# Last part of the FFN down projection: both column halves per pair of tokens instead of half after half

## The chip, the cores and the metric

The kernel runs on one core of a Trainium2 chip. The metric is the device time of one execution in microseconds. The time before is the median of three runs. The profile is one further execution recorded by the hardware profiler; its times are counted from the start of its own span.

## The reference

A trunk of two layers on 512 tokens of 1024 channels in float32. Each layer is a token-mixing sublayer (dilated attention and retention) followed by a SwiGLU FFN, each with a residual and a LayerNorm behind it. What the change touches is the end of the FFN:

```python
D_MODEL, SEQ, DEPTH, D_FF = 1024, 512, 2, 2816
def _swiglu(x, w_gate, w_up, w_down):
    h = silu(x @ w_gate) * (x @ w_up)          # [512, 2816]
    return h @ w_down                          # [512, 1024]
for l in range(DEPTH):
    mix = _hybrid_mixer(x, ...)
    x = _layer_norm(ALPHA * x + mix, ln1_g[l], ln1_b[l])
    x = _layer_norm(ALPHA * x + _swiglu(x, ...), ln2_g[l], ln2_b[l])
```

## The kernel before

Every float32 matrix product is done as three matmuls in a reduced float32 format: each operand is split into a high part and a remainder (`hilo`, L94 to L96: a cast on ACT writes the high part, a subtraction on DVE writes the low part), and `high*high + high*low + low*high` is accumulated in a PSUM tile. Raw weights come by DMA on SP's queue into the pool `raw` of 8 buffers; their parts go to `whi` and `wlo`, 4 buffers each. PSUM has 8 tiles in rotation.

"Token" below means a block of 128 tokens; there are four, 0 to 3. `xtok` holds the residual stream of the four tokens with channels in the free dimension; `xh` and `xl` hold the two parts of the transposed stream, which every projection of the next layer reads.

The FFN runs in three parts of the hidden dimension. Parts 0 and 1 go through a Strassen-like scheme and are not touched. Part 2 has 6 hidden blocks of 128 (`FPARTS` (16, 22)). Its down projection is plain: the hidden values `ht` are stationary, the weights stream 512 columns at a time. One call of `xstat` covers one half of the 1024 columns, 6 blocks x 3 matmuls = 18 matmuls per token, 72 for four tokens. The first half (`hf=0`) reads `whi`/`wlo` and runs weight by weight with four open PSUM tiles; the second half (`hf=1`) reads its weights from `xs`, a buffer that is free by then (`tail_units`), and runs token by token.

After each (token, half) `residual` (L1184, L1186) adds the PSUM tile to `xtok` and takes its statistics. After a token's second half `norm` follows (L1169 to L1175, with `rstd_of`, L134 to L138): aggregate on DVE, a first pass over 1024 columns, a power on POOL (`ry`, L135), three tiny steps on DVE, a second pass over the columns. In the last layer the second pass is in two pieces of 512, each followed by its DMA to `out`. In layer 0 a DMA on POOL's queue spills the token, and two steps of `to_xT` are put into a queue of side work: for each half of the channels four transposes on PE (L193, tile `px`), the cast to `xh` on ACT, the subtraction to `xl` on DVE and a copy to `xc` on ACT.

The side queue is emptied by `tick`, which is called after every three matmuls; at the rate set here one entry leaves for every two ticks, and entries `nothing` are spacers. The next layer begins with four 24-matmul products on tokens 0 and 1 (`wstat_halves`, 256 columns each, 96 matmuls), which need `xh`, `xl` of both tokens and four weight units (`whi`/`wlo` at L95, L96), and then the same on tokens 2 and 3, ahead of which `need` forces the transposes that are still in the queue. Each engine runs its instructions in the order of its own list; a scheduler merges the streams of the program into these lists.

Of the kernel before, what the change touches and what calls it, by code (L numbers as in the profile page):

```python
# [19 lines left out]
P = 128  # L20
# [3 lines left out]
NI = S // P  # L24
# [31 lines left out]
def hybrid_kernel(ctx, tc, x, rel_bias, w_in, b_in, w_attn_proj, w_ret_proj, w_out,  # L56
# [3 lines left out]
    pe, act, dve, pool = nc.tensor, nc.scalar, nc.vector, nc.gpsimd  # L60
# [22 lines left out]
    def mm(ps, a, b, start, stop):  # L83
        pe.matmul(ps, lhsT=a, rhs=b, start=start, stop=stop, skip_group_check=True)  # L84
# [6 lines left out]
    def psum(name="px"):  # L91
        return psm.tile([P, S], F32, tag="mm", name=name)

    def hilo(src, hi, lo):  # L94
        act.copy(out=hi, in_=src)  # L95
        dve.tensor_tensor(out=lo, in0=src, in1=hi.bitcast(F32), op=ALU.subtract)  # L96

    def raw(name="raw"):
        return rawp.tile([P, 1024], F32, tag="raw", name=name)
# [4 lines left out]
    def rows(w):  # L104
        return w.rearrange("(k p) c -> p k c", p=P)

    def view(t, a, b):
        return t[:, :a * b].rearrange("p (a b) -> p a b", a=a)

    def load(src, a, b):  # L110
        v = view(raw(), a, b)
        for v_, s_ in pieces(v, src):
            nc.sync.dma_start(v_, s_)
        return v

    def pieces(v, src):

        if len(src.shape) == 3:
            return [(v, src)]
        n = src.shape[3]  # L120
        return [(v[:, :, g * n:(g + 1) * n], src[:, :, g]) for g in range(src.shape[2])]

    def unit(v):
        a, b = v.shape[1], v.shape[2]
        h = view(wp.tile([P, 1024], F32R, tag="whi", name="whi"), a, b)
        l = view(wp.tile([P, 1024], F32R, tag="wlo", name="wlo"), a, b)
        hilo(v, h, l)
        return h, l
# [26 lines left out]
    side, rate, credit, awaited = deque(), [1.0], [0.0], [0] * NI  # L155

    def tick(us):

        if side:
            credit[0] += rate[0] * us  # L160
            while side and credit[0] >= 1.0:
                credit[0] -= 1.0
                side.popleft()()
# [16 lines left out]
    STEP = 0.68  # L180


    def to_xT(src, i, cp, late=None):


        awaited[i] = 2
        t_ = slice(i * P, (i + 1) * P)

        def one(hf):
            awaited[i] -= 1  # L190
            px = psum()
            for d in range(4):
                pe.transpose(px[:, d * P:(d + 1) * P], src[:, (4 * hf + d) * P:(4 * hf + d + 1) * P], ident)  # L193
            pv = px.rearrange("p (d t) -> p d t", d=4)
            ks = slice(4 * hf, 4 * hf + 4)
            hilo(pv, xh[:, ks, t_], xl[:, ks, t_])
            if cp is not None:
                o_ = cp[i // 2][hf][:, :, (i % 2) * P:(i % 2 + 1) * P]
                if late is None:
                    act.copy(out=o_, in_=pv)  # L200
                else:
                    late.append(lambda: act.copy(out=o_, in_=pv))

        return [lambda hf=hf: one(hf) for hf in range(2)]
# [15 lines left out]
    def x_copies():  # L220
        return [[view(raw("xc"), 4, 256) for _ in range(2)] for _ in range(2)]
# [54 lines left out]
                    tick(STEP / 2)  # L276
        return pss

    def xstat(units, n, st, evict, token_outer=False):

        ks = [(u, kk) for u in units for kk in range(u[0].shape[1])]
        nk = len(ks)

        def one(ps, j, i):
            (h, l), kk = ks[j]
            sh, sl = st(j, i)
            mm(ps, sh, h[:, kk], j == 0, False)
            mm(ps, sh, l[:, kk], False, False)
            mm(ps, sl, h[:, kk], False, j == nk - 1)
            tick(STEP)  # L290

        if token_outer:
            for i in range(NI):
                ps = psum("ps")[:, :n]
                for j in range(nk):
                    one(ps, j, i)
                evict(i, ps)
        else:
            pss = [psum("ps")[:, :n] for _ in range(NI)]
            for j in range(nk):  # L300
                for i in range(NI):
                    one(pss[i], j, i)
                    if j == nk - 1:
                        evict(i, pss[i])

    def tail_units(raws):

        out_ = []
        for j, r in enumerate(raws):
            v = xs[:, j].rearrange("p h k t -> p h (k t)").rearrange("p h (a b) -> p h a b", a=2)  # L310
            hilo(r, v[:, 0], v[:, 1])
            out_.append((v[:, 0], v[:, 1]))
        return out_
# [204 lines left out]
    spill = drp.tile([S, D], F32, name="spill")  # L518
# [167 lines left out]
    def layer(ly, cp):  # L686
# [80 lines left out]
        with stage("attn") as ap_, stage("attw", 4) as aw:  # L767
# [62 lines left out]
            if ly == 0:  # L830
# [33 lines left out]
                cp = x_copies()  # L864
# [3 lines left out]
                pss = [psum("ps") for _ in tiles]  # L868
# [41 lines left out]
            if ly:  # L910
                pss = wstat_halves([(us, j) for us in us0 for j in range(2)])
# [50 lines left out]
            bias, tail = {}, []  # L962
            load_bias(0)
            for hp in range(HPG // 2):
# [21 lines left out]
                tail = t_  # L986
                pace(25 if hp < 2 else 32)
            n = [nothing]
# [8 lines left out]
        with stage("ret") as rp:  # L997
# [139 lines left out]
            for dp in range(KD // 2):  # L1137
                h, l = was[dp]
# [5 lines left out]
                for e in range(2):  # L1144
                    cs = slice(e * P, (e + 1) * P)
                    ps = psum("ps")
# [9 lines left out]
        xt = fp.tile([P, NI, D], F32, name="xtok")  # L1156
# [8 lines left out]
        def norm(i, dst=None):  # L1165
            xi = xt[:, i]
            g_, b_ = lnp
            mv = sm.tile([P, 2], F32, tag="mv", name="mv")
            dve.bn_aggr(out=mv, in_=stats[i])  # L1169
            rs = rstd_of(mv[:, 1:2])  # L1170
            dve.scalar_tensor_tensor(out=xi, in0=xi, scalar=mv[:, 0:1], in1=g_, op0=ALU.subtract, op1=ALU.mult)
            n = D if dst is None else D // 2
            for c in range(0, D, n):
                o_ = xi[:, c:c + n]
                dve.scalar_tensor_tensor(out=o_, in0=o_, scalar=rs, in1=b_[:, c:c + n], op0=ALU.mult, op1=ALU.add)  # L1175
                if dst is not None:
                    nc.sync.dma_start(dst[:, c:c + n], o_)

        def residual(i, hf, ps, first, last):
            o_ = xt[:, i, hf * 512:(hf + 1) * 512]  # L1180
            if first:
                dve.scalar_tensor_tensor(out=o_, in0=o_, scalar=ALPHA, in1=ps, op0=ALU.mult, op1=ALU.add)
            else:
                dve.tensor_tensor(out=o_, in0=o_, in1=ps, op=ALU.add)  # L1184
            if last:
                dve.bn_stats(out=stats[i][:, hf], in_=o_)  # L1186

        with stage("mp") as mp:
# [10 lines left out]
            for dp in range(KD // 2):  # L1199
# [8 lines left out]
                pss = [psum("ps") for _ in range(2)]  # L1208
# [21 lines left out]
            for hf in range(2):  # L1230
# [6 lines left out]
                raws = [load(wo_l[:, k:k + 2, hf * 512:(hf + 1) * 512], 2, 512) for k in range(0, KD, 2)]  # L1237
# [4 lines left out]
        wg_l, wu_l, wd_l = rows(w_ffn_gate[ly]), rows(w_ffn_up[ly]), rows(w_ffn_down[ly])  # L1242
        final = ly == DEPTH - 1
        cp = []
# [107 lines left out]
        for part, (f0, f1) in enumerate(FPARTS):  # L1352
            last = part == len(FPARTS) - 1
            ht = []
            for f in range(f0, f1, 2):
                ht.append(fo.tile([P, 7, 2, 256], F32R, tag="op", name="ht"))
                if f:
                    ffn_pair(f, ht[-1], not last)
                else:
                    ffn_plain(f, ht[-1])  # L1360
                if f == 2:
                    drain()
            rate[0], credit[0] = 0.5 / STEP, 0.0
            if not last:
                down_blocks(f0, f1, ht, part == 0)
                continue
            lt = fo.tile([P, 2 * D], F32, tag="op", name="lnp")
            ln_par(lt, ln2_g[ly], ln2_b[ly])

            def h_tok(k, i):  # L1370
                t, q = ht[k // 2], 2 * (i // 2) + k % 2
                cs = slice(i % 2 * P, (i % 2 + 1) * P)
                return t[:, q, 0, cs], t[:, q, 1, cs]

            for hf in range(2):
                def evd(i, ps, hf=hf):
                    residual(i, hf, ps, False, True)
                    if hf == 1:
                        norm(i, out[i * P:(i + 1) * P] if final else None)
                        if not final:  # L1380
                            pool.dma_start(spill[i * P:(i + 1) * P], xt[:, i])
                            side.extend([nothing] * (6, 2, 4, 5)[i] + to_xT(xt[:, i], i, cp))

                raws = [load(wd_l[:, a:a + 2, hf * 512:(hf + 1) * 512], 2, 512) for a in range(f0, f1, 2)]
                tail = hf == 1
                if tail and not final:
                    cp.extend(x_copies())
                xstat(tail_units(raws) if tail else [unit(r) for r in raws], 512, h_tok, evd, token_outer=tail)
        fin.close()
        return cp  # L1390

# [59 lines left out]
```

## Time and profile before

| what | value |
|---|---|
| median of 3 runs | 2125.46 us (2123.43 to 2128.12) |
| profiled execution | 2125.37 us, span 2123.3 us |
| PE busy | 2096.5 us, 99% of the span |
| DVE, ACT, POOL busy | 1585.6, 1112.6, 258.3 us |
| mean granted TensorE clock | 0.995 |
| layer 0's touched part | about 1022.7 to 1057 us |
| the last layer's touched part | about 2078 to 2111 us, end of the span 2123.3 us |

Rows of the timeline read: start, duration, engine, line, operation, output<-input, shape, count, and in brackets the idle time of that engine just before and what ended it. A row of the windows reads: stretch, its length, then for each engine its busy time and (count), the granted TensorE clock, the share of the DMA engines, GB/s. Starts of successive instructions on DVE lie a little closer than their durations.

### The profile page before, as it was taken

What the parts mean: (1) busy time and instruction counts of PE and PEld (TensorE: products, weight loads), DVE (VectorE), ACT (ScalarE), POOL (GpSimd) and SP (SyncE); (2) the same over time, 40 slices, a digit from 0 to 9 for tenths busy, and PEclk for the clock granted to TensorE, in tenths of its full rate; (3) what the DMA queues carried; (4) which work ended last, traced back from release to release, by engine and by line L of the source; (5) the groups of instructions that cost most, each with busy time, mean ns of one, the idle gap of its engine ahead of it and who ended that gap; (6) DMA issues with size and microseconds to landing.
All of it is one profiled execution on the core that took longest, in us unless ns stands there. A gap on an engine that the chain in (4) does not pass through costs nothing.

```text
span 2123.3 us, 34880 instructions
## 1 busy us (share of the span) xinstructions
PE 2096.5 (99%) x13818; PEld 1902.2 (90%) x13818; DVE 1585.6 (75%) x2275; ACT 1112.6 (52%) x1723; POOL 258.3 (12%) x265
## 2 busy tenths in 40 slices
PE   9999999999999999999999999999999999999997
PEld 8989888889988898989899898888899889989896
DVE  7666888787744798887677578887867357988876
ACT  5567655555623365555255666555666233655551
POOL 4111111101000101111120111111100001110101
PEclk9999999999999999999999999999999999999999
DMA  7865567677776168867258554758687761686861
GB/s 243 210 166 147 128 152 181 180 184 177 229 265 197 43 160 192 196 178 190 80 148 229 140 138 120 183 149 205 168 193 247 235 198 37 173 201 166 205 182 40
DMA packets 319940, 363.91 MB, mean 171 GB/s; under 512 B 22429, under 2 KB 251969, under 8 KB 319648
## 3 DMA queue, kind: packets, MB, share of 16 engines
q1 hardware_dynamic: 229888, 257.20, 38.6%
q0 software_dynamic: 62608, 91.68, 23.1%
q10 hardware_dynamic: 27280, 12.80, 2.1%
q8 instruction: 108, 1.77, 0.3%
q14 instruction: 56, 0.46, 0.1%
HBM read 335.84 MB, written 28.53 MB: 172 GB/s over the span
## 4 chain that ended last, share of the span: by engine, by line
PE 88%; issue 4%; DVE 3%; DMA 2%; ACT 2%; POOL 1%; SPq 0%; POOLq 0%; DVEq 0%; ACTq 0%
PE ps L84 80%; PE px L84 6%; DMA raw<-in_w_in 1%; DVE wlo L360 1%; PE px L585 1%; PE px L1043 1%; ACT whi L354 1%; POOL ry L135 1%; DMA y_d<-yt 0%; PE px L193 0%; ACT s L575 0%; DVE xtok L1175 0%; PE px L650 0%; DMA exd<-pk 0%; DVE raw L376 0%
## 5 line engine op out<-in xcount | busy, mean ns | idle before, releaser
L354 ACT CAST whi<-raw 128x1024 fp32r<-128x1024 f32 (+1 forms) x518 | 519.6, 1008 | 461.8 <-PE ps L84 190.0
L360 DVE TENSOR_TENSOR wlo<-raw,whi 128x1024 fp32r<-128x1024 f32 (+1 forms) x518 | 604.7, 1171 | 207.9 <-ACT whi L354 202.1
L84 PE MATMUL ps<-xs,whi 128*128 128x256 f32 (+1 forms) x2944 | 572.1, 293 | 0.4 <-ACT sn L815 0.4
L84 PEld LDWEIGHTS ps<-xs,whi 128*128 128x128 f32 x2944 | 467.6, 191 | 15.0 <-issue 1.7
L84 PE MATMUL ps<-xs,wlo 128*128 128x256 f32 (+1 forms) x1472 | 430.2, 292 | 0.6 <-DVE wlo L360 0.6
L84 PE MATMUL ps<-xh,whi 128*128 128x256 f32 (+1 forms) x1424 | 423.8, 299 | 5.8 <-ACT whi L95 4.0
L84 PE MATMUL ps<-xh,wlo 128*128 128x256 f32 (+1 forms) x1424 | 419.9, 296 | 2.2 <-DVE wlo L96 2.1
L84 PE MATMUL ps<-xl,whi 128*128 128x256 f32 (+1 forms) x1424 | 420.8, 296 | 0.3 <-DVE ve L134 0.3
L84 PEld LDWEIGHTS ps<-xh,whi 128*128 128x128 f32 x1424 | 272.2, 192 | 19.2 <-ACT whi L95 4.9
L84 PEld LDWEIGHTS ps<-xs,wlo 128*128 128x128 f32 x1472 | 281.7, 191 | 6.1 <-DVE wlo L360 1.1
L84 PEld LDWEIGHTS ps<-xl,whi 128*128 128x128 f32 x1424 | 273.5, 192 | 8.8 <-DVE xl L96 0.6
L84 PEld LDWEIGHTS ps<-xh,wlo 128*128 128x128 f32 x1424 | 272.8, 192 | 9.1 <-DVE wlo L96 2.4
L84 PE MATMUL ps<-whi,xs 128*128 128x512 f32 (+1 forms) x768 | 225.0, 362 | 1.0 <-ACT sn L499 1.0
L345 POOL DMA_DIRECT2D raw<-in_w_in x80 | 98.7, 1248 | 692.2 <-DMA raw<-in_w_in 265.4
L96 DVE TENSOR_TENSOR wlo<-raw,whi 128x1024 fp32r<-128x1024 f32 (+2 forms) x78 | 88.8, 1140 | 125.1 <-ACT whi L95 125.0
L376 DVE TENSOR_TENSOR raw<-raw 128x1024 f32<-128x1024 f32 (+1 forms) x148 | 173.9, 1175 | 8.8 <-DMA raw<-in_w_in 6.7
L84 PE MATMUL ps<-whi,ht 128*128 128x512 f32 x544 | 169.1, 390 | 0.0
L84 PEld LDWEIGHTS ps<-whi,xs 128*128 128x128 f32 x768 | 137.8, 188 | 20.5 <-ACT sn L499 1.2
L95 ACT CAST whi<-raw 128x1024 fp32r<-128x1024 f32 (+2 forms) x78 | 76.4, 982 | 142.8 <-PE ps L84 100.3
L84 PE MATMUL ps<-wlo,xs 128*128 128x512 f32 (+1 forms) x384 | 138.3, 360 | 0.1
L84 PEld LDWEIGHTS ps<-whi,ht 128*128 128x128 f32 x544 | 101.8, 188 | 22.4 <-DVE ht L96 1.5
L345 POOL DMA_DIRECT2D raw<-in_w_ffn_gate x40 | 51.7, 1292 | 528.2 <-DMA raw<-in_w_ffn_up 222.7
(221 smaller groups left out, 2975.8 us busy)
## 6 DMA issues: line engine op xcount, KB each, us to landing
raw<-in_w_in SPq DMA_DIRECT2D x168, 512.0 KB, 5.1
raw<-in_w_in POOLq DMA_DIRECT2D x64, 512.0 KB, 8.2
raw<-in_w_ffn_up SPq DMA_DIRECT2D x64, 512.0 KB, 4.8
raw<-in_w_ffn_down SPq DMA_DIRECT2D x52, 512.0 KB, 4.5
raw<-in_w_ffn_gate SPq DMA_DIRECT2D x44, 512.0 KB, 5.4
raw<-in_w_ffn_gate POOLq DMA_DIRECT2D x40, 512.0 KB, 7.6
raw<-in_w_ret_proj SPq DMA_DIRECT2D x32, 512.0 KB, 6.2
raw<-in_w_in SPq DMA_DIRECT2D x56, 256.0 KB, 5.0
```

Source lines behind the costliest of these rows:

```text
L84: pe.matmul(ps, lhsT=a, rhs=b, start=start, stop=stop, skip_group_check=True)
L95: act.copy(out=hi, in_=src)
L96: dve.tensor_tensor(out=lo, in0=src, in1=hi.bitcast(F32), op=ALU.subtract)
L135: pool.tensor_tensor(out=y, in0=ve, in1=mhalf, op=ALU.pow)
L345: pool.dma_start(r, self.src({"P1": "B12", "P3": "B22"}[n], u), accum_op=ALU.add)
L354: act.copy(out=h, in_=src)
L360: dve.tensor_tensor(out=l, in0=src, in1=h.bitcast(F32), op=ALU.subtract)
L376: dve.tensor_tensor(out=r, in0=r, in1=self.t["B22" if n == "P2" else "B21", u], op=ALU.add)
L585: pe.transpose(px[:, hh, j * P:(j + 1) * P], ss[od][:, hh, j * P:(j + 1) * P], ident)
L1043: pe.transpose(px[:, t * P:(t + 1) * P], ys[i][:, t * P:(t + 1) * P], ident)
```

## The change

`xstat` gets a list of tokens. All six weight loads of both halves are now written ahead of the first matmul, and both sets of units are held through the whole part. The order of (half, tokens) is:

- layer 0: half 0 of tokens 0 and 1 together, half 1 of token 0, half 1 of token 1, half 0 of tokens 2 and 3 together, half 1 of token 2, half 1 of token 3;
- last layer: the same up to token 1, then half 0 and half 1 of token 2, then half 0 and half 1 of token 3.

The number of matmuls, casts, subtractions and DMAs stays. The spacers for tokens 2 and 3 change from 4 and 5 to 6 and 3. The out projection, which calls the same `xstat`, keeps its order.

```diff
-    def xstat(units, n, st, evict, token_outer=False):
+    def xstat(units, n, st, evict, token_outer=False, toks=range(NI)):
...
+        groups = [(i,) for i in toks] if token_outer else [toks]
+        for group in groups:
+            ps = {i: psum("ps")[:, :n] for i in group}
             for j in range(nk):
+                (h, l), kk = ks[j]
+                for i in group:
+                    sh, sl = st(j, i)
+                    mm(ps[i], sh, h[:, kk], j == 0, False)
+                    mm(ps[i], sh, l[:, kk], False, False)
+                    mm(ps[i], sl, h[:, kk], False, j == nk - 1)
+                    tick(STEP)
                     if j == nk - 1:
+                        evict(i, ps[i])
...
-            for hf in range(2):
-                def evd(i, ps, hf=hf):
-                    residual(i, hf, ps, False, True)
...
-                            side.extend([nothing] * (6, 2, 4, 5)[i] + to_xT(xt[:, i], i, cp))
-
-                raws = [load(wd_l[:, a:a + 2, hf * 512:(hf + 1) * 512], 2, 512) for a in range(f0, f1, 2)]
-                tail = hf == 1
-                if tail and not final:
-                    cp.extend(x_copies())
-                xstat(tail_units(raws) if tail else [unit(r) for r in raws], 512, h_tok, evd, token_outer=tail)
+            def evd(hf, i, ps):
+                residual(i, hf, ps, False, True)
+                if hf == 1:
+                    norm(i, out[i * P:(i + 1) * P] if final else None)
+                    if not final:
+                        pool.dma_start(spill[i * P:(i + 1) * P], xt[:, i])
+                        side.extend([nothing] * (6, 2, 6, 3)[i] + to_xT(xt[:, i], i, cp))
+
+            raws = [[load(wd_l[:, a:a + 2, hf * 512:(hf + 1) * 512], 2, 512) for a in range(f0, f1, 2)] for hf in range(2)]
+            units = [[unit(r) for r in raws[0]], tail_units(raws[1])]
+            if not final:
+                cp.extend(x_copies())
+            ends = ((0, (2, 3)), (1, (2,)), (1, (3,))) if not final else ((0, (2,)), (1, (2,)), (0, (3,)), (1, (3,)))
+            for hf, toks in ((0, (0, 1)), (1, (0,)), (1, (1,))) + ends:
+                xstat(units[hf], 512, h_tok, lambda i, ps, hf=hf: evd(hf, i, ps), toks=toks)
```

In the changed file all lines below `xstat` stand 9 lower in number (L1184 becomes L1175, L1175 becomes L1166, L1171 becomes L1162, L1169 becomes L1160). On ACT and DVE the casts and subtractions of all six units stood ahead of the part's first residual before as well, and their rows have not moved; SP's and POOL's lists and ACT's, but for one pair of neighbours, are the same.

On PE, at the end of layer 0, before: the last 72 matmuls on `xs`, with the transposes of token 0 among them and those of token 1 behind them, then layer 1's first matmuls (`xh`, `xl` with `whi`):

```order
L84 MATMUL ps<-whi,ht 128x512
L84 MATMUL ps<-xs,ht 128x512 x60
L193 MATMUL px<-ident,xtok 128x128 x4
L84 MATMUL ps<-xs,ht 128x512 x6
L193 MATMUL px<-ident,xtok 128x128 x4
L84 MATMUL ps<-xs,ht 128x512 x6
L193 MATMUL px<-ident,xtok 128x128 x8
L84 MATMUL ps<-xh,whi 128x256
```

PE at the same place now: these are token 2 (18 matmuls) and token 3 (18), and the transposes are those of token 1; token 0's stand further up, within half 0 of tokens 2 and 3:

```order
L84 MATMUL ps<-wlo,ht 128x512
L84 MATMUL ps<-whi,ht 128x512
L84 MATMUL ps<-xs,ht 128x512 x12
L193 MATMUL px<-ident,xtok 128x128 x4
L84 MATMUL ps<-xs,ht 128x512 x6
L193 MATMUL px<-ident,xtok 128x128 x4
L84 MATMUL ps<-xs,ht 128x512 x18
L84 MATMUL ps<-xh,whi 128x256
L84 MATMUL ps<-xl,whi 128x256
L84 MATMUL ps<-xh,wlo 128x256
```

No transpose is left between the part and layer 1. Token 2's two groups of transposes now stand 48 and 60 matmuls behind layer 1's first one, token 3's behind the 96th; before, token 2's stood behind the 60th and the 72nd.

On DVE, before, from the residual of token 2 (half 1) on, the first weight remainder (`wlo`) of layer 1 comes seven rows below the end of this piece:

```order
L1184 TENSOR_TENSOR xtok<-xtok,ps 128x512
L1186 BN_STATS stats<-xtok 128x6
L96 TENSOR_TENSOR xl<-px,xh 128x4x128
L1169 BN_AGGR mv<-stats 128x2
L134 TENSOR_SCALAR ve<-mv 128x1
L1171 SCALAR_TENSOR_TENSOR xtok<-xtok,mv,lnp 128x1024
L136 SCALAR_TENSOR_TENSOR rt<-ry,ve 128x1
L96 TENSOR_TENSOR xl<-px,xh 128x4x128
L137 TENSOR_SCALAR rt<-rt 128x1
L1184 TENSOR_TENSOR xtok<-xtok,ps 128x512
L138 TENSOR_TENSOR ry<-ry,rt 128x1
L1186 BN_STATS stats<-xtok 128x6
```

DVE now, from the same residual on:

```order
L1175 TENSOR_TENSOR xtok<-xtok,ps 128x512
L96 TENSOR_TENSOR wlo<-raw,whi 128x1024
L96 TENSOR_TENSOR xl<-px,xh 128x4x128
L1177 BN_STATS stats<-xtok 128x6
L96 TENSOR_TENSOR wlo<-raw,whi 128x1024
L1160 BN_AGGR mv<-stats 128x2
L96 TENSOR_TENSOR wlo<-raw,whi 128x1024
L134 TENSOR_SCALAR ve<-mv 128x1
L1162 SCALAR_TENSOR_TENSOR xtok<-xtok,mv,lnp 128x1024
L136 SCALAR_TENSOR_TENSOR rt<-ry,ve 128x1
L1175 TENSOR_TENSOR xtok<-xtok,ps 128x512
L137 TENSOR_SCALAR rt<-rt 128x1
```

All four `wlo` (the fourth follows at once) moved ahead of the end of token 2's norm, one `xl` moved out of it.

On DVE at the end of the last layer, before, the residual of token 3 (the row L1184) stands inside the norm of token 2:

```order
L1171 SCALAR_TENSOR_TENSOR xtok<-xtok,mv,lnp 128x1024
L136 SCALAR_TENSOR_TENSOR rt<-ry,ve 128x1
L1184 TENSOR_TENSOR xtok<-xtok,ps 128x512
L137 TENSOR_SCALAR rt<-rt 128x1
L1186 BN_STATS stats<-xtok 128x6
L138 TENSOR_TENSOR ry<-ry,rt 128x1
L1169 BN_AGGR mv<-stats 128x2
L1175 SCALAR_TENSOR_TENSOR xtok<-xtok,ry,lnp 128x512 x2
L134 TENSOR_SCALAR ve<-mv 128x1
L1171 SCALAR_TENSOR_TENSOR xtok<-xtok,mv,lnp 128x1024
```

DVE there now:

```order
L1162 SCALAR_TENSOR_TENSOR xtok<-xtok,mv,lnp 128x1024
L136 SCALAR_TENSOR_TENSOR rt<-ry,ve 128x1
L137 TENSOR_SCALAR rt<-rt 128x1
L138 TENSOR_TENSOR ry<-ry,rt 128x1
L1166 SCALAR_TENSOR_TENSOR xtok<-xtok,ry,lnp 128x512 x2
L1175 TENSOR_TENSOR xtok<-xtok,ps 128x512
L1177 BN_STATS stats<-xtok 128x6
L1175 TENSOR_TENSOR xtok<-xtok,ps 128x512
L1177 BN_STATS stats<-xtok 128x6
L1160 BN_AGGR mv<-stats 128x2
```

Token 2's norm now ends before the two residuals of token 3 (half 0, then half 1).

More of the change, by code (lines that the diff above doesn't have):

```diff
@@ L277, in wstat_halves @@
         return pss
-    def xstat(units, n, st, evict, token_outer=False):
+    def xstat(units, n, st, evict, token_outer=False, toks=range(NI)):
         ks = [(u, kk) for u in units for kk in range(u[0].shape[1])]
         nk = len(ks)
[L284 to L299, printed above, removed]
-            for j in range(nk):
-                for i in range(NI):
-                    one(pss[i], j, i)
+        groups = [(i,) for i in toks] if token_outer else [toks]
+        for group in groups:
+            ps = {i: psum("ps")[:, :n] for i in group}
+            for j in range(nk):
+                (h, l), kk = ks[j]
[5 more added lines that the diff above has]
+                    tick(STEP)
                     if j == nk - 1:
-                        evict(i, pss[i])
+                        evict(i, ps[i])
     def tail_units(raws):
@@ L1373, in h_tok @@
                 return t[:, q, 0, cs], t[:, q, 1, cs]
-            for hf in range(2):
-                def evd(i, ps, hf=hf):
-                    residual(i, hf, ps, False, True)
[L1378 to L1381, printed above, removed]
-                            side.extend([nothing] * (6, 2, 4, 5)[i] + to_xT(xt[:, i], i, cp))
-                raws = [load(wd_l[:, a:a + 2, hf * 512:(hf + 1) * 512], 2, 512) for a in range(f0, f1, 2)]
-                tail = hf == 1
-                if tail and not final:
-                    cp.extend(x_copies())
-                xstat(tail_units(raws) if tail else [unit(r) for r in raws], 512, h_tok, evd, token_outer=tail)
+            def evd(hf, i, ps):
[12 more added lines that the diff above has]
+                xstat(units[hf], 512, h_tok, lambda i, ps, hf=hf: evd(hf, i, ps), toks=toks)
         fin.close()
```

## The prediction

> **What bounds the kernel now.** I read the page first, then the waits of PE over the whole span:
>
> ```profile
> PE 2096.5 (99%) x13818; PEld 1902.2 (90%) x13818; DVE 1585.6 (75%) x2275; ACT 1112.6 (52%) x1723; POOL 258.3 (12%) x265
> PE ps L84 <- ACT whi L95: 4.0, 1, 4.0
> PE ps L84 <- DVE wlo L96: 2.1, 1, 2.1
> PE px L585 <- DVE nm L572: 1.3, 1, 1.3
> ```
>
> PE is the bound, and of what it lost to others the two longest waits happened once each; the next inside the span, in layer 1's attention, is 1.3 us. The number of matmuls does not change, so time can only come from places where PE stands still, runs at a lower clock, or has finished. The windows show where that is near the touched code:
>
> ```profile
> 1057.00:1061.30 4.30, 0.32 (x3) 0.08 (x1) 3.84 (x9) 2.60 (x5) 0.90 (x1) 1.00 0.00 0
> 1061.30:1068.90 7.60, 5.12 (x21) 4.63 (x22) 7.14 (x13) 4.01 (x5) 2.51 (x3) 0.56 0.45 147
> 2110.00:2116.00 6.00, 0.91 (x4) 0.41 (x3) 5.49 (x15) 0.00 (x0) 1.52 (x1) 0.79 0.23 87
> 2116.00:2123.30 7.30, 0.00 (x0) 0.00 (x0) 3.11 (x6) 0.00 (x0) 1.52 (x1) 0.50 0.39 145
> ```
>
> After the first touched part PE (first busy column) is idle for 4.3 us and then works at a clock of 0.56 while DVE (third) is full. After the second it has ended at about 2110.9 and the rest of the span is DVE's norms and the output. These are the handover and the tail; the change acts on both. The handover in PE's timeline:
>
> ```profile
> 1022.68 0.40 PE L84 MATMUL ps<-whi,ht 128*128 128x512 f32 x1
> 1039.03 13.77 PE L84 MATMUL ps<-xs,ht 128*128 128x512 f32 x60
> 1052.63 0.60 PE L193 MATMUL px<-ident,xtok 128*128 128x128 f32 x4
> 1052.98 1.63 PE L84 MATMUL ps<-xs,ht 128*128 128x512 f32 x6
> 1056.28 1.04 PE L193 MATMUL px<-ident,xtok 128*128 128x128 f32 x8
> 1061.35 0.38 PE L84 MATMUL ps<-xh,whi 128*128 128x256 f32 x1 [4.03 <-ACT whi L95]
> 1073.38 0.28 PE L84 MATMUL ps<-xl,whi 128*128 128x256 f32 x1
> 1073.50 0.28 PE L84 MATMUL ps<-xh,wlo 128*128 128x256 f32 x1
> 1078.81 1.03 PE L193 MATMUL px<-ident,xtok 128*128 128x128 f32 x8
> 1080.08 0.74 PE L84 MATMUL ps<-xh,whi 128*128 128x256 f32 x4 [0.24 <-ACT xh L95]
> ```
>
> 72 matmuls from 1022.68 to 1039.03 make 0.227 us each for 512 columns; a step at 256 columns is 0.12 at full clock; a group of four transposes takes 0.35 (1052.63 to 1052.98). Tokens 2 and 3 of layer 1 begin at 1080.08, which is 1.27 after the last transposes begin. That start is my yardstick: behind it nothing is reordered, and of the waits above only the 1.3 us lies there.
>
> **Part 1: PE up to layer 1.** Layer 0's part keeps its 144 matmuls; now four transpose groups stand inside it. Counting from 1022.68 at 0.227: token 0 ends after 54 matmuls at 1034.9, token 1 after 72 at 1039.0, half 0 of tokens 2 and 3 with two transpose groups at 1047.9, token 2 at 1052.3, token 3 at 1056.8. Before, PE was through at about the same time, 1056.28 plus two groups, so nothing is gained up to here.
>
> **Part 2: tokens 0 and 1 are in time.** A token's residual and norm on DVE, and the passage from transposes to `xl`:
>
> ```profile
> 1043.31 0.69 DVE L1184 TENSOR_TENSOR xtok<-xtok,ps 128x512 f32<-128x512 f32 x1 [1.17 <-PE ps L84]
> 1048.65 0.68 DVE L1184 TENSOR_TENSOR xtok<-xtok,ps 128x512 f32<-128x512 f32 x1
> 1073.62 0.60 PE L193 MATMUL px<-ident,xtok 128*128 128x128 f32 x4
> 1074.26 0.59 ACT L95 CAST xh<-px 128x512 fp32r<-128x512 f32 x1 [6.96 <-PE px L193]
> 1074.87 0.69 DVE L96 TENSOR_TENSOR xl<-px,xh 128x512 fp32r<-128x512 f32 x1 [4.48 <-ACT xh L95]
> 1060.23 1.07 ACT L95 CAST whi<-raw 128x1024 fp32r<-128x1024 f32 x1
> ```
>
> One norm is 5.34 (1043.31 to 1048.65); the residual starts some 0.2 after the matmul (90 matmuls end at 1043.1). Tokens 0 and 1 are normed at 1035.1 + 5.3 = 1040.5 and 1045.8. Their transposes come at 1044.5, 1046.2, 1050.6 and 1052.3, so PE does not wait. From transposes to the cast on ACT pass 0.64, to `xl` 1.25. ACT casts token 1's first half at 1051.3, then the first `whi` at 1051.8 to 1052.9, and copies and casts on. On DVE token 2's residual comes at 1052.5, the first `wlo` (about 1.15 each) at 1053.1 to 1054.2, the last `xl` to 1054.9, statistics, the second `wlo` to 1056.7. Layer 1's first matmul at 1056.8 finds its operands; the second unit is wanted 12 matmuls later. The 4.0 and 2.1 us waits go, and with them the low clock behind them.
>
> **Part 3: what is late next.** Token 2's transposes stand 48 matmuls into layer 1, at 1056.8 + 48 x 0.12 = 1062.5, and PE runs in order. Token 2's norm on DVE:
>
> ```profile
> 1053.99 0.68 DVE L1184 TENSOR_TENSOR xtok<-xtok,ps 128x512 f32<-128x512 f32 x1
> 1060.06 1.27 DVE L1175 SCALAR_TENSOR_TENSOR xtok<-xtok,ry,lnp 128x1024 f32<-128x1024 f32 x1
> 1061.24 0.20 DVE L1169 BATCH_NORM_AGGREGATE mv<-stats 128x2 f32<-128x12 f32 x1
> 1068.04 2.35 DVE L96 TENSOR_TENSOR wlo<-raw,whi 128x1024 fp32r<-128x1024 f32 x2
> ```
>
> Before it took 1053.99 to 1061.3 = 7.3, with two `xl`, token 3's residual and statistics inside. Now it starts at 1052.5, loses one `xl` (0.6) and gains four `wlo` (2.35 for two, 4.7): 1052.5 + 7.3 - 0.6 + 4.7 = 1063.9. PE waits about 1.4 us there. Bounds: 0, if the `wlo` fill DVE's wait for POOL's power inside the chain and the steps lie closer; 3, if each step waits for its `whi` from ACT. I take 1.4, the sum of the rows. Behind the waiting transposes stand only layer 1's matmuls; DVE's next `xl` waits for them, with token 3's second norm pass behind it: two `xl`-like passages at most, until about 1068.3.
>
> Then 0.35 + 12 x 0.12 + 0.35 + 36 x 0.12 = 6.5 bring PE to token 3's transposes at 1070.4, which finds token 3 ready, and 1.27 later, at 1071.7, tokens 2 and 3 begin. **Handover: 1080.08 - 1071.7 = 8.4 us gained**, 9.8 without the stall.
>
> Does the stall cost clock as well? A nearby case:
>
> ```profile
> 1207.06 0.33 PE L585 MATMUL px<-ident,s 128*128 128x128 f32 x1 [1.30 <-DVE nm L572]
> 1207.93 0.93 PE L585 MATMUL px<-ident,s 128*128 128x128 f32 x5 [0.55 <-ACT s L575]
> 1208.00:1212.00 4.00, 4.00 (x24) 0.61 0.00 0
> 1212.00:1216.00 4.00, 4.00 (x38) 0.96 0.44 131
> ```
>
> Waits of 1.30 and 0.55 close together were followed by a clock of 0.61 over 4 us: 4 x 0.39 + 4 x 0.04 = 1.7 us of full clock lost. My stall is single and has dense matmuls on both sides, so I take no loss and keep 1.7 as the upper end. The Trainium skill, "TensorE: Matmul & The Clock Gate", section "What's actually happening", says that the clock is halved only after at least one idle window of about 3.4 us; by that rule my stall would cost itself alone, and the sum would stay. The rows above, with 1.85 us of waits in all, do not bear out so long a threshold, which is why I keep the other end.
>
> **Part 4: the weights held, and the pairs.** With two tokens per weight, each unit is used up in 12 matmuls instead of 24, so the third unit and the last hidden block are wanted at 24 x 0.227 = 5.4 us, the first `xs` unit at 8.2, counted from the first matmul (1022.68, or 2078.08 in the last layer). Their last writers:
>
> ```profile
> 1022.75 1.22 DVE L96 TENSOR_TENSOR xs<-raw,xs 128x1024 fp32r<-128x1024 f32 x1
> 1025.85 0.69 DVE L96 TENSOR_TENSOR ht<-sn,ht 128x512 fp32r<-128x512 f32 x1 [0.69 <-ACT ht L95]
> ```
>
> `ht` is complete at 1026.5, wanted at 1028.1; `xs` at 1024.0, wanted at 1030.9. Nothing waits, cost zero; the cover is 1.6 us. Loads and casts were that early before, so holding them moves no DMA; the next layer's `whi` buffers come free at 1047.9 at the latest instead of 1039, ahead of the cast at about 1051.8. The spacers change only where the transposes stand, and that is counted above.
>
> **Part 5: the tail.** The end of the last layer on DVE, and PE's last matmuls:
>
> ```profile
> 2094.42 16.48 PE L84 MATMUL ps<-xs,ht 128*128 128x512 f32 x72
> 2098.70 0.69 DVE L1184 TENSOR_TENSOR xtok<-xtok,ps 128x512 f32<-128x512 f32 x1 [1.17 <-PE ps L84]
> 2102.84 1.41 DVE L1175 SCALAR_TENSOR_TENSOR xtok<-xtok,ry,lnp 128x512 f32<-128x512 f32 x2
> 2112.97 0.68 DVE L1184 TENSOR_TENSOR xtok<-xtok,ps 128x512 f32<-128x512 f32 x1
> 2118.24 1.42 DVE L1175 SCALAR_TENSOR_TENSOR xtok<-xtok,ry,lnp 128x512 f32<-128x512 f32 x2
> ```
>
> PE gives a token every 4.1 us (18 x 0.227), a norm takes 5.5 (4.14 from the residual to the last pass, and its 1.41), so DVE falls behind: token 3's residual starts at 2112.97, though PE ended at 2110.9, and its chain to the last pass takes 5.27 with token 2's steps inside, against 4.14 for token 0 (2098.70 to 2102.84). Now token 2 ends 36 matmuls ahead of the end, at 2102.6; token 1's norm, begun at 2096.0, is through at 2102.1; token 2's is through at 2108.3, then 1.3 for half 0 of token 3, and DVE waits at 2111.0. The last pass starts at 2111.0 + 4.14 = 2115.1 instead of 2118.24. What follows, two pieces and their DMAs, stays. **Tail: 3.1 us gained.** Bounds: 2.0 (only the late start, the chain stays at 5.27) to 3.2.
>
> **Sum.** 8.4 + 3.1 = 11.5 against the profiled execution of 2125.37 (span 2123.3, 2.07 around it): 2113.9. That execution stands 0.09 below the median, which changes nothing at this size.
>
> **The rivals.**
> - The stall is longer or pulls the clock down. For it: the 1207 rows, and DVE full in the handover. Against it: dense matmuls on both sides. Price 1.7 alone, to 1.6 + 1.7 with the 3 us bound: 2115.6 to 2117.2. Chance 0.25.
> - No stall: 2113.9 - 1.4 = 2112.5. Against it is the sum of DVE's rows. Chance 0.1.
> - The handover does not move, since something other than the norms ends last there (weights of layer 1, say), and only the tail is gained: 2125.4 - 3.1 = 2122.3. For it: PE's wait was ended by `whi`, a weight cast. Against it: in ACT's list this cast stands behind the casts of the transposed tokens, and these come early now. Chance 0.07.
>
> The fourth ends on the other side. The second half of the columns already ran in groups of 18 matmuls, one PSUM tile each; its window (the clock is the third number from the end):
>
> ```profile
> 1039.00:1052.60 13.60, 13.60 (x61) 11.21 (x60) 11.12 (x23) 0.00 (x0) 3.65 (x3) 1.00 0.10 39
> ```
>
> - Slower, by the clock: PE's stream is now cut into 6 and 7 groups. If every group cost a spell like the one at 1208, 13 x 1.7 = 22 us would go and the time would be 2136; it decides from 7 such spells on, which eat the 11.5. Against it is the full clock of this window. Chance 0.03.
>
> The Trainium skill has a rule for this rival on the same page, section "A second HAM failure mode: psum-queue depth-cycling": short idles between groups that cycle through PSUM banks make the clock swing. By it the part might run at changing clocks and the time come near 2136; the window above shows no such thing for groups of that size.
>
> **How the numbers follow.** The forecast with its own range of 2112.9 to 2115.2 has 0.5, the rivals 0.25, 0.1, 0.07 and 0.03, and 0.05 goes to small new waits in both parts, 2116 to 2120. About 0.2% (4.3 us) is what a measurement of this kernel can tell from no change. Faster by more than that, below 2121.2, are all but the last rivals: 0.9; 2122.3 counts as the same: 0.07; slower 0.03. The range 2111.8 to 2117.8 leaves out the cases of 0.07 and 0.03 and most of the small new waits, and adds half a microsecond for the runs' spread.
>
> **What would show it.** Right: in PE's timeline no idle ahead of layer 1's first matmul and a clock of 1.00 from 1057 on; one wait of 1 to 2 us at the transposes of token 2, put down to `xtok` or DVE's L1166; tokens 2 and 3 of layer 1 begin near 1071.7; the last residual starts within 0.3 us of the last matmul and the span ends near 2111.8. Wrong: a wait inside the down projection on `ht` or `xs`, a stall of 3 us or more in the handover, or a clock under 1 behind it; or the handover gain given back by new waits in layer 1.

## The result, and the profile after

The changed kernel takes 2112.22 us in the median (2111.05 to 2115.39, six runs) against 2125.01 for the kernel before on the same occasion; the ratio of the two is 0.9946, with a 95% interval of 0.9936 to 0.9956. A run of the kernel before that took 5851.41 us here, and one of 2550.49 us beside the last experiment, are left out of the ratios. The ratio makes 11.5 us (9.3 to 13.6), where 11.5 were forecast; the plain difference of the medians is 12.8. The time lies in the range. The page's line of busy times, and two of PE's waits, the longest one inside the layers and the one at token 2's transposes:

```profile
PE 2092.2 (99%) x13818; PEld 1898.8 (90%) x13818; DVE 1585.8 (75%) x2275; ACT 1112.6 (53%) x1723; POOL 258.3 (12%) x265
PE px L576 <- DVE nm L563: 1.7, 2, 1.5
PE px L193 <- DVE xtok L1166: 0.7, 1, 0.7
```

The 4.0 and 2.1 us waits on layer 1's first weights are gone; one new wait of 0.7, on token 2's norm, is there. The windows of the handover and of the tail:

```profile
1057.00:1061.30 4.30, 4.27 (x36) 4.06 (x34) 3.84 (x8) 0.00 (x0) 1.03 (x1) 1.00 0.71 219
1061.30:1068.90 7.60, 6.91 (x59) 6.91 (x60) 5.02 (x10) 2.25 (x4) 3.79 (x6) 1.00 0.57 206
2098.00:2104.00 6.00, 3.23 (x15) 2.34 (x13) 4.56 (x8) 0.00 (x0) 0.81 (x1) 1.00 0.23 87
2104.00:2110.40 6.40, 0.00 (x0) 0.00 (x0) 2.25 (x6) 0.00 (x0) 0.71 (x1) 0.70 0.22 83
```

In the stretch where PE was idle it is now busy for 4.27 of 4.30 us, and the clock stays at 1.00 behind it (it was 0.56). PE's timeline through the handover:

```profile
1020.79 0.40 PE L84 MATMUL ps<-whi,ht 128*128 128x512 f32 x1
1042.58 0.60 PE L193 MATMUL px<-ident,xtok 128*128 128x128 f32 x4
1042.93 0.48 PE L84 MATMUL ps<-whi,ht 128*128 128x512 f32 x1
1044.40 0.60 PE L193 MATMUL px<-ident,xtok 128*128 128x128 f32 x4
1050.79 0.60 PE L193 MATMUL px<-ident,xtok 128*128 128x128 f32 x4
1055.36 0.28 PE L84 MATMUL ps<-xh,whi 128*128 128x256 f32 x1
1061.99 0.66 PE L193 MATMUL px<-ident,xtok 128*128 128x128 f32 x4 [0.72 <-DVE xtok L1166]
1068.67 1.03 PE L193 MATMUL px<-ident,xtok 128*128 128x128 f32 x8
1069.94 0.74 PE L84 MATMUL ps<-xh,whi 128*128 128x256 f32 x4 [0.24 <-ACT xh L95]
```

Layer 1 begins (1055.36) right behind the part's last matmul, without a wait in brackets. The yardstick, from the part's first matmul to the start of tokens 2 and 3 in layer 1, is 1069.94 - 1020.79 = 49.15 us; before it was 1080.08 - 1022.68 = 57.40. Token 2's norm on DVE, from its residual to the step behind its last pass:

```profile
1050.99 0.69 DVE L1175 TENSOR_TENSOR xtok<-xtok,ps 128x512 f32<-128x512 f32 x1
1060.67 1.27 DVE L1166 SCALAR_TENSOR_TENSOR xtok<-xtok,ry,lnp 128x1024 f32<-128x1024 f32 x1
1061.85 0.20 DVE L1160 BATCH_NORM_AGGREGATE mv<-stats 128x2 f32<-128x12 f32 x1
```

It takes 10.9 us, most of it other work in between (four `wlo`, one `xl`, token 3's residual and statistics), and ends at 1061.9, when PE's transposes start. The tail, on PE and DVE:

```profile
2068.40 0.40 PE L84 MATMUL ps<-whi,ht 128*128 128x512 f32 x1
2096.99 4.24 PE L84 MATMUL ps<-xs,ht 128*128 128x512 f32 x18
2097.22 1.42 DVE L1166 SCALAR_TENSOR_TENSOR xtok<-xtok,ry,lnp 128x512 f32<-128x512 f32 x2
2101.27 0.69 DVE L1175 TENSOR_TENSOR xtok<-xtok,ps 128x512 f32<-128x512 f32 x1 [1.31 <-PE ps L84]
2105.38 1.42 DVE L1166 SCALAR_TENSOR_TENSOR xtok<-xtok,ry,lnp 128x512 f32<-128x512 f32 x2
```

Token 2's last pass (2097.22) is over before PE ends at 2101.2; DVE then waits for PE (1.31 in brackets), which it did not before, and the last pass follows 4.11 behind the residual instead of 5.27. From the part's first matmul to the end of the span are 2110.4 - 2068.40 = 42.0 us against 2123.3 - 2078.08 = 45.2, where the first matmul before is this row:

```profile
2078.08 0.40 PE L84 MATMUL ps<-whi,ht 128*128 128x512 f32 x1
```

The profiled executions in four stretches, in us, divided at the part's first matmul in layer 0, the start of tokens 2 and 3 in layer 1, and the part's first matmul in the last layer:

| kernel | ahead | handover | layer 1 | tail | span |
|---|---|---|---|---|---|
| before | 1022.7 | 57.40 | 998.0 | 45.2 | 2123.3 |
| changed | 1020.8 | 49.15 | 998.5 | 42.0 | 2110.4 |
| difference | -1.9 | -8.25 | +0.5 | -3.2 | -12.9 |

1.4 us of this pair's 12.9 lie outside the handover and the tail.

### The profile page after: what moved, and what is told of

It is laid out like the page before. It is cut to its first block, busy times and chain, and to the rows that moved or that the text cites. A ratio compares the mean times of both kernels' runs of the same rounds, so it can differ in the third digit from the quotient of the medians.

```text
span 2110.4 us, 34883 instructions
## 1 busy us (share of the span) xinstructions
PE 2092.2 (99%) x13818; PEld 1898.8 (90%) x13818; DVE 1585.8 (75%) x2275; ACT 1112.6 (53%) x1723; POOL 258.3 (12%) x265
## 4 chain that ended last, share of the span: by engine, by line
PE 89%; issue 4%; DVE 2%; DMA 2%; ACT 1%; POOL 0%; SPq 0%; POOLq 0%; ACTq 0%; DVEq 0%
PE ps L84 81%; PE px L84 6%; DMA raw<-in_w_in 1%; PE px L576 1%; DVE wlo L351 1%; PE px L1034 1%; ACT whi L345 1%; PE px L193 0%; DMA mb<-exd 0%; ACT s L566 0%; DMA raw<-in_w_ffn_gate 0%; POOL ry L135 0%; PE px L641 0%; DMA exd<-pk 0%; DVE raw L367 0%
```

## The experiments

My theory was that two separate gains add up: in the handover, tokens 0 and 1 are normed while PE still works on tokens 2 and 3, and in the tail, token 2's norm is over when PE ends. The rivals were a single cause, a gain by the held weights and the pairs as such, and a gain given back inside layer 1.

**The last layer alone.** Layer 0 keeps the old order:

```diff
+            order = ((0, (0, 1, 2, 3)), (1, (0,)), (1, (1,)), (1, (2,)), (1, (3,))) if not final else <as changed>
-                        side.extend([nothing] * (6, 2, 6, 3)[i] + ...)
+                        side.extend([nothing] * (6, 2, 4, 5)[i] + ...)
```

> The new order in the last layer alone; layer 0 keeps half after half with its old spacers. The yardsticks are read from the profile: the handover, from the first matmul of layer 0's last down projection to the first matmul of layer 1 on tokens 2 and 3 (57.4 us before, 49.15 in the changed kernel), and the tail, from the first matmul of the last layer's part to the end of the span (45.2 before, 42.0 changed). Theory (two gains that do not depend on each other): handover 57.4, tail 42.0, time 3.2 us under the kernel before, ratio 0.9985. Rival (the gain has one cause, the handover, and the tail is only the spread between runs): tail 45.2, ratio 1.000.

Measured: ratio 0.9985 (0.9976 to 0.9994), 3.2 us. The marks in PE's timeline, with a span of 2120.1:

```profile
1022.23 0.40 PE L84 MATMUL ps<-whi,ht 128*128 128x512 f32 x1
1079.83 0.74 PE L84 MATMUL ps<-xh,whi 128*128 128x256 f32 x4 [0.24 <-ACT xh L95]
2078.05 0.40 PE L84 MATMUL ps<-whi,ht 128*128 128x512 f32 x1
```

Handover 57.6, tail 42.05: the tail's gain stands by itself.

**Layer 0 alone.** The last layer keeps the old order:

```diff
+            order = <as changed> if not final else ((0, (0, 1, 2, 3)), (1, (0,)), (1, (1,)), (1, (2,)), (1, (3,)))
```

> The new order in layer 0 alone; the last layer keeps half after half. Theory: handover 49.15, tail 45.2, time 8.3 us under the kernel before, ratio 0.9961. Rival (the changed kernel's whole 12.9 us, with the 1.4 us that lie outside the two parts, belongs to this change): 9.7 us, ratio 0.9954. Rival (part of the gain is given back by new waits inside layer 1): the stretch from the second yardstick to the last layer's part over 999.5 us, against 998.0 before and 998.5 changed.

Measured: ratio 0.9964 (0.9950 to 0.9977), 7.6 us with an interval from 4.9 to 10.6, which holds the theory's 8.3 and the first rival's 9.7 alike; the stretches decide. Span 2112.8:

```profile
1020.93 0.40 PE L84 MATMUL ps<-whi,ht 128*128 128x512 f32 x1
1070.08 0.74 PE L84 MATMUL ps<-xh,whi 128*128 128x256 f32 x4 [0.24 <-ACT xh L95]
2067.72 0.40 PE L84 MATMUL ps<-whi,ht 128*128 128x512 f32 x1
```

Handover 49.15, layer 1 997.6, tail 45.1. Layer 1 is no longer than before, so nothing beyond the spread of its length (last section) is given back there, and 8.25 + 3.2 = 11.45 is the sum of the two.

**The pairs swapped in layer 0.** Tokens 2 and 3 first, 0 and 1 last; the groups and the time for which weights are held stay:

```diff
+            for hf, toks in (<as changed> if final else
+                             ((0, (2, 3)), (1, (2,)), (1, (3,)), (0, (0, 1)), (1, (0,)), (1, (1,)))):
```

> The changed kernel with the pairs swapped in layer 0: tokens 2 and 3 first, tokens 0 and 1 last, all else the same, the weights held as long. Theory (the gain of the handover is that tokens 0 and 1, which layer 1 reads first, are normed while PE still works on the others): it is lost and more, PE idles some 12 us ahead of layer 1 and runs at half clock behind it, handover 62 (59 to 65), against 57.4 before. Rival (the gain is that of holding the weights and of groups by pairs): 49 to 52.

Measured: one run, 2126.23, beside 2127.27 of the kernel before. PE's marks:

```profile
1021.75 0.40 PE L84 MATMUL ps<-whi,ht 128*128 128x512 f32 x1
1062.03 1.94 PE L193 MATMUL px<-ident,xtok 128*128 128x128 f32 x8 [5.55 <-DVE mv L1160]
1068.73 1.97 PE L193 MATMUL px<-ident,xtok 128*128 128x128 f32 x8 [4.76 <-DVE xtok L1166]
1070.53 1.01 PE L84 MATMUL ps<-xh,whi 128*128 128x256 f32 x3
2082.34 0.40 PE L84 MATMUL ps<-whi,ht 128*128 128x512 f32 x1
```

PE waits 5.55 and 4.76 us for the norms of tokens 0 and 1, and the mean clock from 1058 to 1070 is 0.54. No transposes mark the start of tokens 2 and 3 here. Counted in PE's list, the 97th matmul of layer 1 starts at 1083.06, which makes the handover 61.3. Taken from the other side, 1060.6 us pass from the first part's first matmul to the last part's, against 1055.4 before and 1047.6 changed, so with some 998 for layer 1 it is about 62.5. Either is longer than before and within what was expected. The held weights and the pairs are not the gain; which tokens end first is.

**Token 2's transposes 12 matmuls later.** In layer 1's products `tick` counts half, so one spacer is worth 12 matmuls there and not six.

```diff
-                        side.extend([nothing] * (6, 2, 6, 3)[i] + ...)
+                        side.extend([nothing] * (6, 2, 7, 2)[i] + ...)
```

> The changed kernel with one spacer more ahead of token 2's transposes and one less ahead of token 3's, which puts token 2's transposes 60 and 72 matmuls into layer 1 instead of 48 and 60. Theory (PE's stall there is only the order of PE's list against the end of token 2's norm): the wait on the norm goes, handover 48.2 to 48.4. Rival (DVE is the bound of the whole handover, and the wait reappears at token 3's transposes): handover 49.1 with a wait at the 96th matmul.

```profile
1019.54 0.40 PE L84 MATMUL ps<-whi,ht 128*128 128x512 f32 x1
1061.30 0.60 PE L193 MATMUL px<-ident,xtok 128*128 128x128 f32 x4
1067.76 0.74 PE L84 MATMUL ps<-xh,whi 128*128 128x256 f32 x4 [0.24 <-ACT xh L95]
```

The wait is gone and the handover is 48.22 (one run, 2109.88 us). The stall comes from the place of these transposes in PE's list, ahead of the end of token 2's norm.

**Token 2's transposes 24 matmuls earlier.**

```diff
-                        side.extend([nothing] * (6, 2, 6, 3)[i] + ...)
+                        side.extend([nothing] * (6, 2, 4, 5)[i] + ...)
```

> The changed kernel with two spacers less ahead of token 2's transposes (4 instead of 6) and two more ahead of token 3's: token 2's transposes now stand 24 and 36 matmuls into layer 1, 2.9 us earlier on PE, while token 2's norm ends when it did. Theory: PE's single stall there grows from 0.9 to 3.8 us; if a stall of that length leaves the clock alone, the handover is 52.0 us (49.15 + 2.9); if the clock falls to a half for one spell as behind the 1.30 and 0.55 us waits (1.7 us lost), 53.7. Rival (the stall is another engine's work that moves with the transposes): handover 49.2.

PE's marks and its windows (busy, count, clock, DMA share, GB/s) of one run, 2119.53 us:

```profile
1023.88 0.40 PE L84 MATMUL ps<-whi,ht 128*128 128x512 f32 x1
1065.17 0.85 PE L193 MATMUL px<-ident,xtok 128*128 128x128 f32 x4 [3.69 <-DVE mv L1160]
1077.52 0.74 PE L84 MATMUL ps<-xh,whi 128*128 128x256 f32 x4 [0.24 <-ACT xh L95]
1064.00:1066.00 2.00, 0.83 (x5) 0.86 0.78 212
1066.00:1068.00 2.00, 2.00 (x12) 0.50 0.81 308
1068.00:1070.00 2.00, 2.00 (x15) 0.79 0.03 12
```

Handover 53.64, the figure for a spell of low clock. It is 4.49 longer than in the changed kernel, and the longer stall (3.69 against 0.72) makes 2.97 of that. The other 1.5 go with the low clock behind the stall, for which the windows allow at most 2 x (0.14 + 0.50 + 0.21) = 1.7 us. That is what the first rival of the prediction would have cost. The change did not pay it: in none of the four profiles with a stall of 0.7 at this place is the clock under 1 behind it.

**The last layer's order in layer 0.**

```diff
+            order = ((0, (0, 1)), (1, (0,)), (1, (1,)), (0, (2,)), (1, (2,)), (0, (3,)), (1, (3,)))
```

> The changed kernel with the last layer's order in layer 0 as well: half 0 and half 1 of token 2, then half 0 and half 1 of token 3. Token 2 ends 36 matmuls ahead of the end, and its norm on DVE stands ahead of layer 1's four weight remainders instead of behind them. Theory (the stall is those four subtractions in the norm): no wait at token 2's transposes, handover 48.2 to 48.5. Rival (the remainders are now late and PE waits for them at layer 1's start): handover 49.5 to 51 with a wait on wlo.

```profile
1023.23 0.40 PE L84 MATMUL ps<-whi,ht 128*128 128x512 f32 x1
1060.25 0.38 PE L84 MATMUL ps<-xh,wlo 128*128 128x256 f32 x1 [0.63 <-DVE wlo L96]
1072.32 0.74 PE L84 MATMUL ps<-xh,whi 128*128 128x256 f32 x4 [0.24 <-ACT xh L95]
PE ps L84 <- ACT sn L490: 1.7, 1, 1.7
```

Handover 49.09 (one run, 2117.62 us). The wait at the transposes is gone as the theory has it, but the rival was right that another takes its place, 0.63 on a weight remainder that now stands behind the norm. Neither had the size: 48.2 to 48.5 was too low, 49.5 to 51 too high. I had summed DVE's rows for token 2 alone there and had not asked what its norm pushes back. One of the two, the norm or the remainders, is late on DVE in either order. This run's layer 1 is 1001.2 us long, with a wait of 1.7 in its value projection (last row); see the last section.

**Layer 0's order in the last layer.**

```diff
+            ends = ((0, (2, 3)), (1, (2,)), (1, (3,)))
```

> The changed kernel with layer 0's order in the last layer too: half 0 of tokens 2 and 3 together, then half 1 of token 2, half 1 of token 3. Token 2 now ends 18 matmuls (4.1 us) ahead of the end instead of 36, less than a norm's 5.5. Theory (the tail is set by the norm of token 2 still running when PE ends): token 3's last residual starts about 1.5 us after PE's end, tail 43.5 (43.2 to 43.8). Rival (the tail is set by PE's end alone): 42.0.

PE's first matmul of the part, token 3's residual and the last pass, span 2112.6 (one run, 2114.65 us):

```profile
2069.19 0.40 PE L84 MATMUL ps<-whi,ht 128*128 128x512 f32 x1
2103.43 0.68 DVE L1175 TENSOR_TENSOR xtok<-xtok,ps 128x512 f32<-128x512 f32 x1
2107.54 1.41 DVE L1166 SCALAR_TENSOR_TENSOR xtok<-xtok,ry,lnp 128x512 f32<-128x512 f32 x2
```

Tail 43.4. The residual starts 34.24 behind the first matmul, against 32.87 in the changed kernel, where it waits for PE: 1.4 late, because 4.1 us between the last two tokens are less than a norm. So of the tail's 3.2 us, 1.8 come with the order by pairs already: the residual starts 0.65 earlier than before (34.89), and the chain to the last pass takes 4.11 instead of 5.27. The other 1.4 come from finishing token 2 whole ahead of token 3.

**The two best, timed on one chip.** The spacer of 7, and the changed kernel again:

> The changed kernel with token 2's transposes 12 matmuls later, as before, now timed. Theory: handover 48.2 and tail 42.0 in the profile again, 0.9 us better than the changed kernel in its profile and about 12.4 us (9.2 in the handover, 3.2 in the tail) under the kernel before, ratio 0.9942. Rival (what the handover gains comes back inside layer 1): ratio 0.9946 or more with the stretch inside layer 1 over 999 us.

> The changed kernel itself, on the same chip as the last one, so that the two can be compared: handover 49.1, tail 42.0, ratio 0.9946, which is 11.5 us. Theory: the 1.4 us by which the first comparison of profiles came out larger are the spread of layer 0's attention stage between executions, so that the time from the start to layer 0's last down projection lies between 1019 and 1024 us in this run as well and has nothing to do with the kernel.

Measured: 0.9940 (0.9928 to 0.9952) and 0.9939 (0.9927 to 0.9951). The second figure makes 13.0 us (10.4 to 15.5) of the change that made 11.5 on the first occasion, so the ratios fix its gain to some 2 us either way. In the profiles the handover is 48.22 and 49.14, the tail 41.9 and 42.0, the stretch ahead 1021.9 and 1021.8, layer 1 998.5 and 996.9. The spacer's 0.9 us is there in the handover in both of its profiles; in the time it cannot be told from nothing. The handover, the tail and the stretch ahead are as the theories have them, layer 1 stays under the rival's 999, and either expected ratio lies within its interval; the ratios alone would not tell theory and rival apart.

## Why the prediction was right

- PE up to layer 1 (part 1): counted 34.1 us from the part's first matmul to layer 1, measured 34.57. The difference stems from the four groups of transposes inside the part: a group takes 0.35 (1042.58 to 1042.93) as counted, but the six matmuls behind it take 1.47 (to 1044.40) instead of 6 x 0.227 = 1.36.
- Tokens 0 and 1 in time (part 2): held, no wait ahead of layer 1's first matmul.
- What is late next (part 3): named at the right place and by its cause. Token 2's norm was to end 41.2 us after the part's first matmul and ended 1061.9 - 1020.8 = 41.1 after it. That end came out by two errors that cancel: the norm started 0.4 later than counted and took 0.5 less. The stall was 0.7, under the 1 to 2 that were to show the prediction right, since PE arrived 0.6 later than counted. This does not reach the handover, because PE goes on when the norm ends, however early it arrives: 49.0 counted and 49.15 measured, a gain of 8.25 for 8.4.
- The clock: no spell of low clock, as taken. The run with a stall of 3.69 shows that the rival was a real one, and its price, 1.5 measured for 1.7. The reason given for taking none, a single stall with dense matmuls on both sides, is not borne out (see below this list). A stall of the 1.4 that was counted is tested by no run, so that the clock stayed at 1.00 is in part luck.
- The weights held and the pairs (part 4): no wait on `ht` or `xs`, cost zero. The swapped pairs show that they bring nothing of their own either.
- The tail (part 5): 3.2 measured for 3.1, and its two terms, the late start and the interleaved chain, are seen in the rows.
- The sum: both halves were measured alone, 3.2 us by ratio and 8.25 by stretches. The profiled pair differs by 12.9 because of 1.4 us in layers 0 and 1, which change from execution to execution. That the ratio gives the forecast 11.5 to the tenth is luck, with intervals this wide; the stretches are what bears the sum out.

What a wait of 1 to 2 us does to the clock differs from execution to execution. Layer 1's attention has the same two waits close together in all eleven profiles, one of 0.9 to 1.75 us and one of 0.55. Behind them the clock was 0.5 for 3.41 us in four (the kernel before, the first profile of the spacer of 7, layer 0's order in the last layer, the pairs swapped), and 1.00 in the other seven, the changed kernel's among them. These are the two profiles of the kernel with the spacer of 7, each with the first of the two waits and PE's window around them (busy, count, clock, DMA share, GB/s):

```profile
1194.77 0.33 PE L576 MATMUL px<-ident,s 128*128 128x128 f32 x1 [1.10 <-DVE nm L563]
1194.00:1202.00 8.00, 6.68 (x46) 0.79 0.10 27
1199.14 0.33 PE L576 MATMUL px<-ident,s 128*128 128x128 f32 x1 [1.75 <-DVE nm L563]
1198.00:1206.00 8.00, 6.31 (x55) 1.00 0.05 6
```

The longer wait cost no clock and the shorter one did. And in the run with the last layer's order in layer 0, a single wait of 1.7 us on `sn`, with matmuls on both sides, was followed by a clock of 0.5 from 1141.76 for 3.41 us.

The Trainium skill, "TensorE: Matmul & The Clock Gate", section "What's actually happening", names about 3.4 us of idle as the point from which the clock is halved. The stalls of 0.72 (no loss) and 3.69 (a loss) agree with it. The waits above, far shorter, lost clock in some executions all the same, so I would not rely on a single stall's length.

The Trainium skill, "TensorE: Matmul & The Clock Gate", section "A second HAM failure mode: psum-queue depth-cycling", has it that short idles between groups of matmuls that cycle through PSUM banks make the clock swing. Of that nothing is seen here. In the windows of the changed kernel the clock is 1.00 through both parts:

```profile
1020.80:1055.30 34.50, 34.50 (x162) 28.57 (x161) 23.83 (x41) 9.19 (x14) 4.22 (x4) 1.00 0.11 42
2068.40:2101.00 32.60, 32.60 (x146) 26.85 (x144) 22.70 (x43) 1.24 (x2) 4.57 (x3) 1.00 0.13 49
```

## What to carry to other kernels

Where one stage ends in a per-token chain on another engine that is longer than the token's matmuls, order the stage so that the tokens which the next stage reads first are finished entirely while the matmuls of the others still run; no work is saved, and the stall at the border goes. Then look at what comes next in each engine's list: one spacer more or two less decide whether the in-order engine stands still for 0, 0.7 or 3.7 us, and the one run with a stall of the last kind lost clock on top. When the gain is below the spread of the runs, measure it between two marks in the trace, around the changed code.

## What the runs showed that I had not expected

The spread between executions sits outside the handover and the tail. The stretch ahead of layer 0's part took 1019.5 to 1023.9 us over nine further profiles, and layer 1 996.9 to 1001.2, without order by kernel. Compared matmul by matmul over all eleven profiles, PE's starts drift apart by up to 4.4 us in the first 220 us of the execution, and by under 0.6 us from there to the part. PE's wait on ACT's copy `sn` (L490, L499 before) in layer 1's value projection was 0 to 1.7 us in the nine, longest in the run with the longest layer 1. Spells of half clock, 3.41 us each, have a share in it as well: the longest stretch ahead has one from 154.08, behind two waits in layer 0's attention, and the longest layer 1 has the one from 1141.76. Whether waits and spells together are all of the spread, and what delays that copy, stays open. The handover itself repeated within 0.01 us in the four profiles of kernels with the same layer 0 (49.14 to 49.15), and within 0.2 in the two with the old one (57.40 and 57.60).
